# Row-wise infinity norm: the bulk loads move from SyncE's queue to GpSimd's, one packet per DMA engine

## The chip, the core and the metric

The kernel runs on one core of one Trainium2 chip. The metric is device time in microseconds (us) of one execution; lower is better. The core has a tensor, a vector (DVE), a scalar (ACT), a GpSimd (POOL) and a sync (SP) engine, and 16 DMA engines that move data between the memory of the chip (DRAM, HBM) and the on-chip memory of 128 partitions. Any of SP, ACT and POOL can issue a transfer; each of them feeds a queue of its own to the same 16 DMA engines.

## The reference

```
x: 8192 x 8192 float32, normally distributed
out = np.linalg.norm(x, ord=np.inf, axis=1)     # 8192 float32: max |x| of each row
```

Each of the 8192 output values is the largest absolute value of one row of 32 KB. The input is 268.4 MB, the output 32 KB.

## The kernel before

The rows are divided in two parts. Each partition has 64 rows in all; 48 of them are the bulk (`x_b`) and 16 are the tail (`x_t`, `n_tail` = 16).

**The bulk** (lines 65 to 72) is 24 loads, 6 (`A`) times 4 (`G`). Each fills one tile `t` of 128 partitions x 16384 float32: two whole rows per partition, 64 KB that lie together in DRAM, 8.39 MB in all. The load is issued by SP (line 68). One DVE instruction, `reduce_max` with absolute value (line 63, called from line 69), then reduces the tile to two values per partition in `r_bulk`. When all are done, ACT stores `r_bulk` (line 73).

**The tail** (lines 75 to 98) takes the other 16 rows of each partition, two rows (`B`) to a tile `t`, so 8 tiles. The list `TAIL` (lines 17 to 22) says in which pieces each row is loaded: 8 rows whole (32 KB per partition and piece), 5 rows in halves (16 KB), 2 rows in quarters (8 KB), and the last row in three quarters, one piece of 4 KB and two of 2 KB. That is 32 loads, all issued by SP (line 82), each followed by a DVE reduction of its piece (line 94 or 97, again through line 63) into `part` or, for the last row, into spare columns at the end of the tile. Before the last piece's own reduction DVE folds `part` into `r_tail` (line 87), which ACT stores (line 88). The last reduction (line 91) yields `r_fin`, which SP stores (line 99).

**What sets the order.** The tiles `t` of both parts come from one pool with three buffers (`BUFS` = 3, line 51). A load into a buffer waits for the reduction of what the buffer held: load number i waits for the reduction of tile i-3. The first tail tile therefore waits for bulk tile 21 (counting from 0), the second for bulk tile 22, and so on. Besides that, the framework signals the end of the DMAs issued by SP and ACT through eight semaphores in turn, and a DMA also waits until the previous user of its semaphore has landed. Instructions of one engine are issued in the order of the program: on SP all 24 bulk loads come ahead of the 32 tail loads.

In the text, T0 to T23 are the bulk tiles and R0 to R15 the tail rows. The loads of R0 and R1 fill one buffer, those of R2 and R3 the next.

Of the kernel before, what the change touches and what calls it, by code (L numbers as in the profile page):

```python
# [1 line left out]
logging.getLogger("concourse").setLevel(logging.ERROR)  # L3

# [1 line left out]

# [4 lines left out]

F32 = mybir.dt.float32
X = mybir.AxisListType.X

TAIL = (
    [[8192]] * 8
    + [[4096, 4096]] * 5
    + [[2048] * 4] * 2  # L20
    + [[2048, 2048, 2048, 1024, 512, 512]]
)


@with_exitstack
def kernel(
    ctx: ExitStack,
    tc: tile.TileContext,
    x: bass.AP,
    out: bass.AP,  # L30
    G: int = 4,
    B: int = 2,
    BUFS: int = 3,
):
    nc = tc.nc
    P = nc.NUM_PARTITIONS
    rows, cols = x.shape


    n_tail = len(TAIL)  # L40
    assert n_tail % B == 0
    n_bulk_rows = rows // P - n_tail
    assert n_bulk_rows % (G * B) == 0
    A = n_bulk_rows // (G * B)
    split = n_bulk_rows * P
    x_b = x[:split].rearrange("(a p n b) c -> a n p (b c)", p=P, a=A, n=G, b=B)
    out_b = out[:split].rearrange("(a p n b) -> p a (n b)", p=P, a=A, n=G, b=B)
    x_t = x[split:].rearrange("(p t b) c -> t p (b c)", p=P, b=B)
    out_t = out[split:].rearrange("(p t) -> p t", p=P)

    sbuf = ctx.enter_context(tc.tile_pool(name="sbuf", bufs=BUFS))
    outp = ctx.enter_context(tc.tile_pool(name="outp", bufs=1))

    k_last = len(TAIL[-1])
    r_bulk = outp.tile([P, A, G * B], F32)
    r_tail = outp.tile([P, n_tail], F32)
    r_fin = outp.tile([P, 1], F32)
    k_max = max(len(r) for r in TAIL[:-1])
    part = outp.tile([P, n_tail - 1, k_max], F32)
    nc.vector.memset(part[:], 0.0)  # L60

    def absmax(o, i):
        nc.vector.reduce_max(out=o, in_=i, axis=X, apply_absolute_value=True)  # L63

    for a in range(A):
        for n in range(G):
            t = sbuf.tile([P, B * cols + 16], F32, tag="t")
            nc.sync.dma_start(out=t[:, : B * cols], in_=x_b[a, n])  # L68
            absmax(
                r_bulk[:, a, n * B : (n + 1) * B],  # L70
                t[:, : B * cols].rearrange("p (b c) -> p b c", b=B),
            )
    nc.scalar.dma_start(out=out_b, in_=r_bulk[:])

    for i in range(0, n_tail, B):
        t = sbuf.tile([P, B * cols + 16], F32, tag="t")
        for j in range(B):
            r = i + j
            at = j * cols
            last = r == n_tail - 1  # L80
            for k, w in enumerate(TAIL[r]):
                nc.sync.dma_start(  # L82
                    out=t[:, at : at + w], in_=x_t[i // B][:, at : at + w]
                )
                if last and k == k_last - 1:

                    absmax(r_tail[:, : n_tail - 1], part[:])
                    nc.scalar.dma_start(
                        out=out_t[:, : n_tail - 1], in_=r_tail[:, : n_tail - 1]
                    )  # L90
                    absmax(r_fin[:], t[:, at : B * cols + k_last - 1])
                elif last:
                    absmax(
                        t[:, B * cols + k : B * cols + k + 1], t[:, at : at + w]
                    )
                else:
                    absmax(part[:, r, k : k + 1], t[:, at : at + w])
                at += w
    nc.sync.dma_start(out=out_t[:, n_tail - 1 :], in_=r_fin[:])


# [1 line left out]
_INS = ['x']  # L103
_OUTS = [((8192,), 'float32')]


# [23 lines left out]
```

## Time and profile before

| | us |
|---|---|
| median of 3 runs (629.82 to 629.88) | 629.88 |
| the profiled execution's own time | 629.88 |
| its span, first to last instruction | 628.1 |
| time around the span (629.88 - 628.1) | 1.78 |
| DVE busy | 552.7 |
| one bulk reduction (128x2 from 128x16384), 24 of them | 17.219 |
| one tail reduction of a whole row (128x8192), 8 of them | 8.677 |
| one tail reduction of half a row (128x4096), 10 of them | 4.412 |
| median of a bulk load from issue to landing | 40.7 |

The profile is that of one execution. A page of it gives the busy time of each engine, the span in 40 slices, the DMA queues (q1 carries what SP issues, q10 what ACT issues), and the chain of work that ended last, followed backwards. Other views are the timeline (instructions in order of time, with the idle time of the engine before each and what ended it), the waits (who waited for whom) and windows (rates and busy times in chosen stretches). The trace also holds a record of every DMA packet, with queue, size, start and length. `L63` is line 63 of the kernel; "SPq" is SP issuing a DMA. Input and tile names stand as `out<-in`.

### The profile page before, as it was taken

The page shows a single profiled execution, that of the slowest core. Times are in us where ns is not written, and L with a number is a line of the kernel's source. Part 1 is how long each engine was busy: PE and PEld are TensorE (multiplying, and loading weights), DVE is VectorE, ACT ScalarE, POOL GpSimd, SP SyncE. Part 2 cuts the span into 40 slices and gives each one's busy share as a digit, 9 for nine tenths or more (in the row PEclk, how much of TensorE's full clock was granted, in tenths as well). Part 3 has the DMA queues.
Part 4 walks back from the last instruction along what each step waited for, and adds up shares of the span by engine and source line. Part 5 has one row for each costly group of instructions (what it writes and reads, how often), then busy time and mean ns, then how long its engine had stood idle before and what let it go on. Part 6 is the DMA issues. An engine that isn't in the chain of part 4 may idle for free.

```text
span 628.1 us, 196 instructions
## 1 busy us (share of the span) xinstructions
DVE 552.7 (88%) x58; POOL 0.2 (0%) x4
## 2 busy tenths in 40 slices
DVE  0588988889988889888898888998889999999998
POOL 0000000000000000000000000000000000000000
DMA  9999999999999999999999999999999999999996
GB/s 401 413 455 413 455 413 455 413 455 413 455 413 455 409 459 413 455 413 455 413 455 413 455 413 455 413 455 413 455 405 430 434 435 432 420 432 432 424 426 274
DMA packets 9138, 268.49 MB, mean 427 GB/s; under 512 B 1968, under 2 KB 1968, under 8 KB 2352
## 3 DMA queue, kind: packets, MB, share of 16 engines
q1 hardware_dynamic: 8208, 268.44, 99.1%
q10 hardware_dynamic: 928, 0.03, 0.1%
q14 instruction: 2, 0.02, 0.0%
HBM read 268.44 MB, written 0.03 MB: 427 GB/s over the span
## 4 chain that ended last, share of the span: by engine, by line
DMA 64%; DVE 30%; another core or an unknown queue 4%; issue 1%; SPq 0%
DMA t<-in_x_dram 64%; DVE r_bulk L63 23%; DVE part L63 5%; DVE t L63 1%; SPq L82 0%; DVE r_fin L63 0%; SPq L68 0%
## 5 line engine op out<-in xcount | busy, mean ns | idle before, releaser
L63 DVE TENSOR_REDUCE r_bulk<-t 128x2 f32<-128x16384 f32 x24 | 413.3, 17219 | 70.5 <-DMA t<-in_x_dram 70.5
L63 DVE TENSOR_REDUCE part<-t 128x1 f32<-128x4096 f32 (+2 forms) x26 | 130.0, 5067 | 1.3 <-DMA t<-in_x_dram 1.3
L63 DVE TENSOR_REDUCE t<-t 128x1 f32<-128x2048 f32 (+2 forms) x5 | 8.6, 1746 | 0.4 <-DMA t<-in_x_dram 0.4
L60 DVE MEMSET part<- 128x60 f32 x1 | 0.1, 108 | 0.8 <-PEq L114 0.8
L63 DVE TENSOR_REDUCE r_fin<-t 128x1 f32<-128x517 f32 x1 | 0.7, 692 | 0.0
L63 DVE TENSOR_REDUCE r_tail<-part 128x15 f32<-128x60 f32 x1 | 0.2, 216 | 0.0
L114 POOL MEMSET const-bfloat16-1.0<- 128x1 bf16 x1 | 0.1, 101 | 0.0
L114 POOL MEMSET const-uint8-127<- 128x1 uint8 x1 | 0.1, 101 | 0.0
L114 POOL MEMSET const-float32-0.0<- 128x1 f32 x1 | 0.1, 98 | 0.2 <-issue 0.2
L114 POOL MEMSET const-float32-1.0<- 128x1 f32 x1 | 0.1, 98 | 0.0
## 6 DMA issues: line engine op xcount, KB each, us to landing
t<-in_x_dram SPq DMA_DIRECT2D x8, 4096.0 KB, 37.0
t<-in_x_dram SPq DMA_DIRECT2D x10, 2048.0 KB, 30.4
t<-in_x_dram SPq DMA_DIRECT2D x11, 1024.0 KB, 24.6
t<-in_x_dram SPq DMA_DIRECT2D x1, 512.0 KB, 15.9
t<-in_x_dram SPq DMA_DIRECT2D x2, 256.0 KB, 13.2
t<-in_x_dram SPq DMA_DIRECT2D x24, 40.7
out_dram<-r_bulk ACTq DMA_DIRECT2D x1, 24.0 KB, 57.9
out_dram<-r_tail ACTq DMA_DIRECT2D x1, 7.5 KB, 5.6
```

The source lines that it names most:

```text
L60: nc.vector.memset(part[:], 0.0)
L63: nc.vector.reduce_max(out=o, in_=i, axis=X, apply_absolute_value=True)
L114: nc = _bacc.Bacc("TRN2", target_bir_lowering=False, num_devices=1)
```

## The change

Line 68, the load of the bulk, is issued by GpSimd in place of SP, and with the option `single_packet=True`. The option asks that all descriptors that one DMA engine gets of one load (here those of 8 partitions) make one packet. Nothing else is edited: the tail loads stay on SP, the stores stay where they are, the shapes, the buffers and the reductions are the same.

```
     for a in range(A):
         for n in range(G):
             t = sbuf.tile([P, B * cols + 16], F32, tag="t")
-            nc.sync.dma_start(out=t[:, : B * cols], in_=x_b[a, n])
+            nc.gpsimd.dma_start(
+                out=t[:, : B * cols], in_=x_b[a, n], single_packet=True
+            )
             absmax(
                 r_bulk[:, a, n * B : (n + 1) * B],
                 t[:, : B * cols].rearrange("p (b c) -> p b c", b=B),
```

More of the change, by code (lines that the diff above doesn't have):

```diff
@@ L67 @@
             t = sbuf.tile([P, B * cols + 16], F32, tag="t")
-            nc.sync.dma_start(out=t[:, : B * cols], in_=x_b[a, n])
+            nc.gpsimd.dma_start(
+                out=t[:, : B * cols], in_=x_b[a, n], single_packet=True
+            )
             absmax(
```

## The prediction

> **What bounds the kernel now.** I read the page first: span and engines, the slices, the queues, the chain.
>
> ```profile
> span 628.1 us, 196 instructions
> DVE 552.7 (88%) x58; POOL 0.2 (0%) x4
> ...
> GB/s 401 413 455 413 455 413 455 413 455 413 455 413 455 409 459 413 455 413 455 413 455 413 455 413 455 413 455 413 455 405 430 434 435 432 420 432 432 424 426 274
> ...
> q1 hardware_dynamic: 8208, 268.44, 99.1%
> q10 hardware_dynamic: 928, 0.03, 0.1%
> ...
> DMA 64%; DVE 30%; another core or an unknown queue 4%; issue 1%; SPq 0%
> ```
>
> Look at q1: one queue keeps the 16 DMA engines busy for 99.1% of the span, and the rate is level from the second slice to the last but one. DVE is 88% busy, so it has slack, but only 75 us in 628. The transfers are the bound. The bulk is read from the timeline, whose last column says what DVE waited for:
>
> ```profile
> 0.73 116.98 SPq L68 DMA_DIRECT2D t<-in_x_dram  x8
> ...
> 22.83 17.22 DVE L63 TENSOR_REDUCE r_bulk<-t 128x2 f32<-128x16384 f32 x1 [21.91 <-DMA t<-in_x_dram]
> 42.11 17.22 DVE L63 TENSOR_REDUCE r_bulk<-t 128x2 f32<-128x16384 f32 x1 [2.06 <-DMA t<-in_x_dram]
> ```
>
> DVE starts each tile when it lands and then idles about 2.1 us. The hand-over to the tail is in the same view:
>
> ```profile
> 428.83 17.22 DVE L63 TENSOR_REDUCE r_bulk<-t 128x2 f32<-128x16384 f32 x1 [2.14 <-DMA t<-in_x_dram]
> 446.07 165.44 SPq L82 DMA_DIRECT2D t<-in_x_dram  x32
> 448.11 17.22 DVE L63 TENSOR_REDUCE r_bulk<-t 128x2 f32<-128x16384 f32 x1 [2.06 <-DMA t<-in_x_dram]
> 467.49 17.22 DVE L63 TENSOR_REDUCE r_bulk<-t 128x2 f32<-128x16384 f32 x1 [2.15 <-DMA t<-in_x_dram]
> 484.62 60.23 DVE L63 TENSOR_REDUCE part<-t 128x1 f32<-128x8192 f32 x7
> ```
>
> T23 starts on DVE at 467.49, T0 at 22.83: 444.66 / 23 = 19.333 us per load of 8.389 MB, 433.9 GB/s. SP issues the first tail load at 446.07, just as T21's reduction frees its buffer (428.83 + 17.22), while T22 is landing and T23 is queued. After T23 DVE is the late one for a while: it goes from 484.62 without a gap through seven rows.
>
> How DVE's lateness is worked off: R0's packets end at 476.7 (packet records), DVE takes it at 484.6, so it is 7.9 us behind; the rows land 9.7 us apart and take 8.68, about 1 us regained per row, so at R7 DVE waits again. Behind T23 DVE idles only 0.38 + 0.56 + 0.38 + 0.15 + 0.20 = 1.7 us until it ends at 625.74. That 1.7 us is all the lateness that T23 can gain without moving the end.
>
> **The rates in windows**, for what a packet costs (last column GB/s: the bulk, then pieces of 32, 16 and 8 KB):
>
> ```profile
> 177.48:254.73 77.25, 68.88 (x4) 0.00 (x0) 1.00 1.00 434
> ...
> 488.00:540.00 52.00, 52.00 (x7) 0.00 (x0) 1.00 1.01 434
> 550.00:590.00 40.00, 39.44 (x10) 0.00 (x0) 1.00 1.01 432
> 594.00:619.00 25.00, 24.81 (x12) 0.00 (x0) 1.00 1.01 426
> ```
>
> The packet records say the same more finely. Each bulk load is 128 packets of 64 KB, 8 per engine, of 2.418 us each; 32 KB packets take 1.213. Twice 1.213 less 2.418 leaves 8 ns that a packet (or a descriptor, here the same) costs beyond its bytes.
>
> **Part 1: issue moves from SP to POOL.** 24 issues of 0.328 us (7.9 us) and their 21 waits for buffers leave SP for POOL, whose own work is four memsets of 0.1 us that end at 0.43. In steady state nothing of it is on the path: a load is issued 40.7 us before it lands, 19.3 of which are its own transfer and some 20 the queue ahead. POOL may take up to 20 us per load before a DMA engine runs dry. POOL's slowness would have to pass that cover, 60 times SP's row, to cost anything.
>
> A rule that speaks against it: the Trainium skill ("SBUF — State Buffer", the box on DVE blocking DMA) says that GpSimd can't write its descriptors while DVE runs a two-port fast mode. The 17.219 us for 16384 elements, 1.05 ns each, look like one element per step, and no row here shows such a lock. Were it held for a whole reduction, 17.2 us would still lie within the cover.
>
> The first load has no cover. SP issues it at 0.73, its first packet starts at 1.75 (records): 1.02 us. No row shows POOL doing this. From below: 0, it is as fast. From above: three loads are issued back to back, and if POOL prepares all before the first moves, three times SP's 1.02, so +2.0. I take +1.0, twice SP's time, because descriptors now come from a program. It shifts every landing, the end too: all of it is on the path.
>
> The skill's page "DMA: Bandwidth & Descriptors" (Specifications) gives about 1 us to the first byte for GpSimd's path and 0.6 for SP's; by that the term would be +0.4 and the forecast 629.6.
>
> **Part 2: one packet per engine.** Eight packets become one. If the 8 ns belong to the packet, 7 x 8 ns x 24 loads = 1.3 us go; if to the descriptor, none. Bounds of the bulk's rate: at best -1.3 (the bytes alone set the rest). At worst, the lowest rate that a full queue shows here, 426 GB/s of the 8 KB pieces: 24 x 19.333 = 464.0 us x (434/426 - 1) = +8.7. The nearest row is the bulk's own, same bytes, same runs, so I stay by it and take the middle of 0 and -1.3, -0.65.
>
> Against it speaks the skill's same page (Latency and other measured facts): engines 7 and 15 are usually slower, with a guess that descriptor rings in on-chip memory, which only GpSimd's path has, load their ports. In this trace all 16 engines finish each load within 0.9 us of each other (T23: 466.2 to 467.0), with no drift over 24 loads; there is no such ring here, and no row prices it.
>
> **Part 3: two queues meet at the hand-over.** Before, R0 stood behind T23 in one queue. Now T23 waits in POOL's queue and R0 in SP's. How the engines share is visible in the bulk's store on ACT (L73): issued at 484.74, 57.9 us to landing. It has 6 x 128 runs of 32 bytes and 16 semaphore writes, 49 small packets per engine; 57.9 / 49 = 1.18 us, one 32 KB packet of SP between any two. The engines alternate packet by packet. So T23 as one packet, once begun, can't be cut. The engines begin it between 446.83 and 447.68; SP's R0, issued at 446.07, is there 1.02 later, 447.09, when 10 of 16 have begun T23. On the others one packet of R0, 1.21 us, may pass first. T23 is then 1.2 us late, within the 1.7 us. Cost 0. SP's later loads are released by DVE as before, and SP's longest wait behind the store (23.2 us, to 542.66) has cover: the engines have work until 544.8 + 4.8 (R8's first half) = 549.6, less 1.02 for the issue, so 5.9 us. Stores, reductions and the end don't change.
>
> **Sum.** Against the profiled run's own 629.88 (628.1 + 1.78 around it; equal to the median): +1.0 - 0.65 + 0 = +0.35, 630.2. Its own range: -1.3 + 0 to 0 + 2.0, 628.6 to 631.9.
>
> **Rivals.**
> - *Interleaving (slower).* The option doesn't act, as each load has 128 descriptors in all, or each descriptor stays a packet. Place: 447. T23's eight packets alternate with R0's and R1's: 8 x 2.42 + 8 x 1.21 = 29.0 us in place of 19.3, so T23 is 9.7 us late; if two packets are already begun, 7.3. Less DVE's 1.7 us of idle: +5.6 to +8.0. With +1.0 for the start and no packet gain: 636.5 to 638.9. It decides once T23 lands over 1.7 us late. For it: the store shows strict alternation. Against: the option is meant for this, and 8 descriptors per engine are few.
> - *A lower rate on GpSimd's queue (slower).* From 432 to 426 GB/s over the bulk, the 16 and 8 KB rows: +2.1 to +8.7, plus 1.0: 633 to 639.6. For it: no row shows this queue. Against: equal bytes and runs, and engines that are already the limit.
> - *The full packet gain with a quick start (faster).* -1.3 + 0: 628.6, hardly beyond what can be told. Nothing in the profile allows more, as start, 268 MB and end stay.
>
> **Numbers.** A measurement of this kernel tells from no change about 0.2%, 1.26 us. Forecast 0.50 (faster 0.03, same 0.33, slower 0.14, as its upper end passes 631.1), faster rival 0.15 (0.10 beyond the bound, 0.05 within), lower rate 0.20, interleaving 0.15. Faster 0.13, same 0.38, slower 0.49. Signs are mixed, so the likeliest case's own range, 628.6 to 631.9, stands beside the whole: 628.5 to 637.5, which cuts the upper ends of the two slow rivals.
>
> **What would show it.** A queue of POOL's with 201.3 MB, q1 with 67.1. First reduction at 23.8 in place of 22.83 (start). Reductions 19.28 us apart if the packet gain is full, 19.33 if none, above that a slow queue. T23's start on DVE 19.3 us after T22's, and idle time behind it as before; with interleaving 27 to 29 us after, and no DVE idle to the end. I am wrong if POOL's first issue costs several us, if one DMA engine lags, or if DVE's tail loses its gaps.

## The result, and the profile after

The changed kernel takes **639.1 us** (639.01 to 639.29) against 629.88: ratio 1.0145, 95% interval 1.0127 to 1.0163, so 9.2 us slower. The forecast was 630.2 with a range to 637.5. The profiled execution took 639.08.

The page of the changed kernel, the same parts as were shown of before:

```profile
span 637.0 us, 204 instructions
DVE 552.1 (87%) x58; POOL 13.0 (2%) x28
...
GB/s 383 407 461 416 440 444 412 461 395 461 444 412 461 395 461 444 412 461 395 461 432 424 457 399 461 420 436 449 426 409 428 414 430 428 422 429 430 423 426 89
...
q0 software_dynamic: 3456, 201.33, 73.1%
q1 hardware_dynamic: 4752, 67.11, 24.7%
...
DMA 53%; DVE 46%; issue 1%; DVEq 0%; PEldq 0%
```

The bulk's 201.3 MB now go through a queue of their own, q0. The rate stays as level as before, and DVE has no more work. Yet DVE's share of the chain that ended last has gone from 30% to 46%: the end is now set by DVE, not by the transfers. The last slice, 89 GB/s, says the same: most of it passes after the last load has landed.

The timeline shows where that came from (last column: DVE's idle time and what ended it):

```profile
1.25 1.70 POOL L68 DMA_DIRECT2D t<-in_x_dram  x3 [0.80 <-PEq L127]
23.70 17.22 DVE L63 TENSOR_REDUCE r_bulk<-t 128x2 f32<-128x16384 f32 x1 [22.77 <-DMA t<-in_x_dram]
...
446.98 167.25 SPq L84 DMA_DIRECT2D t<-in_x_dram  x32
449.01 17.22 DVE L63 TENSOR_REDUCE r_bulk<-t 128x2 f32<-128x16384 f32 x1 [2.06 <-DMA t<-in_x_dram]
478.34 8.69 DVE L63 TENSOR_REDUCE part<-t 128x1 f32<-128x8192 f32 x1 [12.11 <-DMA t<-in_x_dram]
486.95 17.21 DVE L63 TENSOR_REDUCE r_bulk<-t 128x2 f32<-128x16384 f32 x1
504.07 121.04 DVE L63 TENSOR_REDUCE part<-t 128x1 f32<-128x8192 f32 x25
```

Three things are to be seen. The first reduction starts 0.87 us later (23.70, was 22.83). From T0 to T22 the spacing is (449.01 - 23.70) / 22 = 19.332 us, as before. Then, at the hand-over, DVE idles 12.11 us where it idled 2.15, and takes a tail row (R0) ahead of T23; after that it works without a gap to the end.

The account: +0.87 (start) + 9.96 (12.11 - 2.15) - 1.67 (the gaps behind T23 that are gone) = 9.16. DVE's work is 0.6 shorter, the part behind its last reduction 0.26 longer (637.0 - 634.38, was 628.1 - 625.74) and the time around the span 0.30 longer, which makes 9.1 in all; 9.2 were measured.

The packet records of one DMA engine (rebuilt by joining each packet's end to the next one's start; POOL's packets of 64 KB as P, SP's of 32 KB as S, start times) show why T23 is late:

```
445.4 P  447.8 P  450.2 P  452.6 S  453.8 P  456.2 S  457.4 P  459.9 S  461.1 P  463.5 S ...
```

The first packet is T22's last, the next two are T23's, and from then on R0 and T23 take turns (on six of the 16 engines after one packet of T23). T23's packets end at 476.40; 19.33 us behind T22's (448.58) they would have ended at 467.9.

### The profile page after: what moved, and what is told of

It is laid out like the page before. It is cut to its first block, busy times and chain, and to the rows that moved or that the text cites. A ratio compares the mean times of both kernels' runs of the same rounds, so it can differ in the third digit from the quotient of the medians.

```text
span 637.0 us, 204 instructions
## 1 busy us (share of the span) xinstructions
DVE 552.1 (87%) x58; POOL 13.0 (2%) x28
## 3 DMA queue, kind: packets, MB, share of 16 engines
q0 software_dynamic: 3456, 201.33, 73.1%
## 4 chain that ended last, share of the span: by engine, by line
DMA 53%; DVE 46%; issue 1%; DVEq 0%; PEldq 0%
DMA t<-in_x_dram 53%; DVE r_bulk L63 24%; DVE part L63 20%; DVE t L63 1%; DVE r_fin L63 0%; DVE r_tail L63 0%; DVEq L63 0%; PEldq L127 0%
## 5 line engine op out<-in xcount | busy, mean ns | idle before, releaser
L68 POOL DMA_DIRECT2D t<-in_x_dram x24 | 12.8, 533 | 415.2 <-DVE r_bulk L63 414.4
```

What stands on the lines that cost most here:

```text
L68: nc.gpsimd.dma_start(out=t[:, : B * cols], in_=x_b[a, n], single_packet=True)
```

## The experiments

**Theory after this result:** two queues share each DMA engine descriptor by descriptor, whatever the option says; T23 lands 8 to 10 us late; the tail gives DVE no slack to make it up. **Rivals:** the option itself costs; the swapped order on DVE costs; GpSimd's queue is slower in itself; any hand-over costs this.

### e1: without the option

```
-            nc.gpsimd.dma_start(out=..., in_=x_b[a, n], single_packet=True)
+            nc.gpsimd.dma_start(out=..., in_=x_b[a, n])
```

> The changed kernel without the one-packet option; nothing else differs. Theory (the option doesn't keep T23 whole, two queues share an engine descriptor by descriptor whatever it says): 639.1 within 0.4 us, T23's last packet at 476.4, R0 and T23 alternating, DVE idle 12.1 us ahead of R0, reductions 19.33 us apart. Rival (the option itself costs or saves, in the rate of the bulk or at the hand-over): more than 1 us away from 639.1, another spacing of the reductions or another end of T23's packets.

Measured 639.15 us (ratio 1.0147, 1.0132 to 1.0163). T23's packets end 27.80 us after T22's, in the changed kernel 27.82; DVE idles 12.08:

```profile
478.55 8.69 DVE L63 TENSOR_REDUCE part<-t 128x1 f32<-128x8192 f32 x1 [12.08 <-DMA t<-in_x_dram]
```

The option changes nothing that these runs can tell.

### e2: T23 ahead of R0 on DVE

```
+    with tc.issue_after(last_bulk.ins):     # DVE's tail work behind T23's reduction
         for i in range(0, n_tail, B):
```

> The changed kernel, with DVE made to reduce T23 ahead of R0 as in the kernel before; the two queues still share the engines at the hand-over. Theory (T23 lands 8.5 us late because R0 and T23 alternate): DVE starts T23 at about 476.9, 9.4 us later than before, and the end comes 1.5 us ahead of the changed kernel's: 637.6. Rival (the swapped order on DVE is what costs, the sharing is nearly harmless): 631 to 632.

Measured 638.95 us (1.0145, 1.0128 to 1.0162). Its hand-over in the timeline:

```profile
448.84 17.22 DVE L63 TENSOR_REDUCE r_bulk<-t 128x2 f32<-128x16384 f32 x1 [2.08 <-DMA t<-in_x_dram]
477.90 17.22 DVE L63 TENSOR_REDUCE r_bulk<-t 128x2 f32<-128x16384 f32 x1 [11.84 <-DMA t<-in_x_dram]
```

T23 starts 29.06 us after T22, 9.73 late, and that alone makes the time (630.72 of e7, where nothing shares, + 9.73 - 1.67 = 638.8); the order on DVE, which the framework's scheduler had turned by itself, adds nothing that these runs can tell (639.1 and 638.95). My 637.6 was 1.3 too low: T23's packets end at 476.23, but the four bytes that signal its end are written until 477.45. In the records that write takes a turn of its own: it comes behind another packet of SP's, of 1.21 us.

### e3 and e4: one load held back, a failed test

```
+                if r == 0:     # R0's load waits for T22's reduction
+                    tc.add_manual_dep(ld.ins, bulk_red[-2].name, <wait>)
```

> The changed kernel, with R0's load made to wait until DVE has reduced T22 (one tile later than its buffer is free), so that T23 isn't cut; DVE's order stays swapped, R0 ahead of T23. If the swapped order alone is enough: T23's packets end at 468, R0's at about 478, DVE idles some 12 us until R0 and the time is 638.5 to 639.5, as if nothing had been undone. If the sharing alone is the cause: 631.

> Both undone: R0's load waits for T22's reduction, and DVE reduces T23 ahead of R0. The loads of the bulk are still on GpSimd with the one-packet option. Theory (only the hand-over and the start cost): T23 starts on DVE at 468.4, 19.3 us after T22, the engines pause under 0.5 us between T23 and R0, and the time is 629.9 + 0.9 (start) + up to 0.5 = 630.8 to 631.3. Rival (GpSimd's queue costs something by itself, in rate or in the tail): above 632.

Measured 639.12 (e3; 1.0146, 1.0131 to 1.0161) and 638.66 us (e4; 1.0139, 1.0124 to 1.0154). In both, SP still issues a tail load at the old time (446.90 and 447.00): R0 and R1 share a buffer, the scheduler put R1's load ahead, and it shared the engines in R0's place. T23 starts at 478.12 in e4. Neither run undid the sharing, so neither speaks on the theory.

### e5: both loads held back

```
-                if r == 0:
+                if r <= 1:
```

> As e3, but both loads that share the first tail buffer, R0's and R1's, wait until DVE has reduced T22 (in e3 and e4 only R0's waited, R1's was issued ahead of it at 447 and shared the engines in its place, so neither was a test of the sharing). The scheduler then puts T23 ahead of R0 on DVE by itself. Theory (the sharing at the hand-over is what costs): SP's first issue at 466.3, T23 starts on DVE at 468.4, DMA engines pause under 0.5 us, DVE's idle gaps in the tail come back, 629.9 + 0.9 (start) + 0 to 0.5 = 630.8 to 631.3. Rival (GpSimd's queue costs by itself, in its rate or in what follows it): above 632, towards 639.

Measured 633.78 us (1.0059, 1.0042 to 1.0076): over half of the loss is gone, but it is 2.5 above the upper end of what I expected. Timeline:

```profile
466.23 148.84 SPq L86 DMA_DIRECT2D t<-in_x_dram  x32
468.34 17.22 DVE L63 TENSOR_REDUCE r_bulk<-t 128x2 f32<-128x16384 f32 x1 [2.14 <-DMA t<-in_x_dram]
485.48 43.05 DVE L63 TENSOR_REDUCE part<-t 128x1 f32<-128x8192 f32 x5
529.29 8.69 DVE L63 TENSOR_REDUCE part<-t 128x1 f32<-128x8192 f32 x1 [0.77 <-DMA t<-in_x_dram]
```

T23 is on time, and DVE's gaps in the tail are back, larger than before: the transfers bind again, but late ones. In windows (DMA share and GB/s last) the two stretches behind T23's end, first here, then in e7 (one queue, below):

```profile
466.00:470.00 4.00, 1.86 (x2) 0.00 (x0) 1.00 0.72 254
470.00:474.00 4.00, 4.00 (x1) 0.00 (x0) 1.00 0.90 385
```

```profile
466.00:470.00 4.00, 1.86 (x2) 1.04 (x2) 1.00 0.84 360
470.00:474.00 4.00, 4.00 (x1) 0.00 (x0) 1.00 0.99 426
```

SP issues at 466.23, the first packet of R0 starts at 467.25, and the engines finish T23 from 466.96 on: some ran dry. The packet records say how much: all engines have finished T23 by 467.9, the last one begins R0 only at 469.5, at least 1.6 us later, and the first packets take 1.3 to 2.3 us in place of 1.21. A row needs all 16 engines; R7's packets end at 548.4, in e7 at 545.65. The loss is that of the last engine: its start 1.7 us late (in e7 the last one begins R0 at 467.8) and its first packet up to 1.1 us longer, 2.8 of the 3.4 us by which the two profiled executions differ (634.04 and 630.66). So e5 shows that T23 is on time without the sharing, and that most of what is left is the price of the wait that I put in.

### e6: hand-over in the middle of the bulk

```
+            if a < 3:
                 nc.gpsimd.dma_start(..., single_packet=True)
+            else:
+                nc.sync.dma_start(out=t[:, : B * cols], in_=x_b[a, n])
```

> The first 12 bulk loads on GpSimd with the option, the other 12 and the tail on SP: the hand-over is at T11 and T12, in the middle of the bulk. Theory (what costs is DVE's lateness, and only where it can't be worked off): T11 lands 17 to 19 us late since its packets alternate with T12's of equal size, DVE is then that much behind, regains 2.1 us per tile and is on time again by about T21, the engines stay busy: 629.9 + 0.9 (start) + 0 to 1 = 630.8 to 631.8. Rivals: any hand-over between two queues costs its 8 to 10 us, 639 or more; GpSimd's queue costs in proportion to what it loads, 634 to 635.

Measured 634.03 us (1.0067, 1.0052 to 1.0082). Timeline, T10, then T11 with the seven tiles behind it, then T19:

```profile
216.90 17.22 DVE L63 TENSOR_REDUCE r_bulk<-t 128x2 f32<-128x16384 f32 x1 [2.07 <-DMA t<-in_x_dram]
255.79 137.10 DVE L63 TENSOR_REDUCE r_bulk<-t 128x2 f32<-128x16384 f32 x8 [21.67 <-DMA t<-in_x_dram]
393.63 17.22 DVE L63 TENSOR_REDUCE r_bulk<-t 128x2 f32<-128x16384 f32 x1 [0.73 <-DMA t<-in_x_dram]
```

T11 is 19.5 us late (236.26 in e7), twice the lateness of T23, and DVE works it off within eight tiles: here lateness costs nothing by itself. What it does cost is the cover of one load: T14's waits for T11's reduction (273.0), and T13's packets end from 273.65 to 274.5. Engines run dry again (four begin T14 only at 276.1 to 276.5), and T23 starts at 470.94, in e7 at 468.26. So my bound of 1 us was too low, by the same effect as in e5. That GpSimd's queue costs by bytes loaded would fit this time too; e7 rules that out.

### e7: all loads on GpSimd

```
-                nc.sync.dma_start(out=t[:, at : at + w], in_=x_t[...])
+                nc.gpsimd.dma_start(out=t[:, at : at + w], in_=x_t[...])
```

> All loads, the tail's too, on GpSimd, so one queue and no hand-over. Theory: T23 starts 19.3 us after T22, the tail as before, 629.9 + 0.9 = 630.8 to 631.5 (0.533 us of POOL per issue are hidden). Rival (GpSimd's queue itself is slower): 634 and up, and more than in e6.

Measured **630.72 us** (1.0013, 1.0004 to 1.0023). One queue, and the loss is gone but for the start:

```profile
448.90 17.22 DVE L63 TENSOR_REDUCE r_bulk<-t 128x2 f32<-128x16384 f32 x1 [2.06 <-DMA t<-in_x_dram]
468.26 17.22 DVE L63 TENSOR_REDUCE r_bulk<-t 128x2 f32<-128x16384 f32 x1 [2.14 <-DMA t<-in_x_dram]
485.40 60.23 DVE L63 TENSOR_REDUCE part<-t 128x1 f32<-128x8192 f32 x7
546.11 43.35 DVE L63 TENSOR_REDUCE part<-t 128x1 f32<-128x8192 f32 x9 [0.48 <-DMA t<-in_x_dram]
```

This is the timeline of before, 0.8 us later line by line. GpSimd's queue is as fast as SP's, in bulk and in small pieces.

### e8: hand-over one tile later

```
-                nc.sync.dma_start(
+                (nc.gpsimd if i == 0 else nc.sync).dma_start(     # R0, R1 on GpSimd
```

> The changed kernel, with R0's and R1's loads on GpSimd too, so that the hand-over comes one tile later: R0 and R1 share the engines with R2 and R3, and T23 is whole. Theory: R0 lands 7.3 to 9.7 us late, at 485.4 to 488.3, but DVE is busy with T23 until 485.5 in any case, so DVE loses 0 to 2.8 us and has 1.7 to give: 629.9 + 0.9 + 0 to 1.1 = 630.8 to 631.9. Rival (the lateness of the load counts in full wherever the hand-over is): 637 and up.

Measured 640.98 us (1.0176, 1.0161 to 1.0191), 9 above my expectation. Timeline from T23 on:

```profile
468.19 17.22 DVE L63 TENSOR_REDUCE r_bulk<-t 128x2 f32<-128x16384 f32 x1 [2.14 <-DMA t<-in_x_dram]
486.43 8.69 DVE L63 TENSOR_REDUCE part<-t 128x1 f32<-128x8192 f32 x1 [1.02 <-DMA t<-in_x_dram]
505.80 121.05 DVE L63 TENSOR_REDUCE part<-t 128x1 f32<-128x8192 f32 x25 [10.69 <-DMA t<-in_x_dram]
```

R0 came as I had worked out (486.4). I had followed R0 alone: R1 stands behind it in the same queue and shares with R3, so DVE waits 10.69 us for R1. The theory's own sum holds: 630.72 (e7) + 1.02 + 10.69 - 1.67 = 640.8.

### e9 and e10: T23 in small descriptors, with and without the option

Both start from e2. `last` is true for T23; `max_dma_last_dim` is the most bytes that a descriptor may move.

```
             nc.gpsimd.dma_start(
                 out=t[:, : B * cols], in_=x_b[a, n],
+                single_packet=True,      # e10: not on T23
+                max_dma_last_dim=16384 if last else 65536,
             )
```

> As e2 (T23 ahead of R0 on DVE), with only T23's load made of descriptors of 16 KB in place of 64, 32 per engine, and with the one-packet option on it. If the option makes an engine's share one packet that isn't cut: T23 lands within about 1 us of its time, 631 to 632. If the option doesn't bear on how two queues share an engine: as e10. Something between, near 639: a packet is bounded by its bytes (64 KB).

> As e9 without the option on T23's load. Theory (the engines alternate descriptor by descriptor): each of T23's 32 descriptors of 0.61 us is followed by one of SP's of 1.21, R0 to R3 pass ahead of T23's end, T23's packets end at about 502 in place of 468, DVE idles from 466 to then and ends 33 to 34 us later than with one queue: 663 to 666. Rival (the engines share by bytes, or by load): as the changed kernel, near 639.

Measured 661.33 us (e9; 1.0498, 1.0467 to 1.0528) and 660.81 (e10; 1.0489, 1.0459 to 1.052). T23's start on DVE, e9 and then e10:

```profile
500.79 17.22 DVE L63 TENSOR_REDUCE r_bulk<-t 128x2 f32<-128x16384 f32 x1 [33.87 <-DMA t<-in_x_dram]
```

```profile
499.99 17.22 DVE L63 TENSOR_REDUCE r_bulk<-t 128x2 f32<-128x16384 f32 x1 [33.87 <-DMA t<-in_x_dram]
```

The same bytes in four times as many descriptors make T23 not 9.7 but 32 us late: each descriptor of 0.61 us lets one of 1.21 pass. The turns go by descriptor, not by bytes or loads, and the option makes no difference: DVE's wait is the same to the hundredth. The two profiled executions (661.55 and 660.79) are 0.76 us apart, and T22 already starts 0.80 apart (449.70 and 448.90), ahead of the hand-over.

The time of e10 is 2.2 below my expectation of 663 to 666: T23's packets end at 498.31, where I had put 502. I had let one of SP's packets follow each of the 32 descriptors, but the first four or five of an engine passed before SP's first packet was there (450.33).

### e11 and e12: T23 as four small loads, with and without the option

These too start from e2.

```
+            step = 4 if last else 1
+            for h in range(step):
+                nc.gpsimd.dma_start(out=t[h::step, ...], in_=x_b[a, n][h::step],
+                                    single_packet=True)      # e12: not on T23
```

> As e2, with T23's load split in four loads of every fourth partition, 32 descriptors of 64 KB each (2 per engine), the one-packet option on each: the option's limit, if it counts the descriptors of the whole load (128 in the changed kernel), is no longer passed. If the option then keeps an engine's two descriptors together: two of T23's packets in a row for each of R0's, T23 is 4 to 5 us late in place of 8.5 to 9.7, 633 to 635. Theory (no effect on the sharing): strict alternation, 638.5 to 640.

> As e11 without the option on T23's four loads: strict alternation, T23 8.5 to 9.7 us late, 638.5 to 640. If it isn't near the changed kernel's time, the four loads cost something by themselves, and e11 is to be read against this one.

Measured 641.66 us (1.0183, 1.0153 to 1.0212) and 641.88 (1.0186, 1.0157 to 1.0216). T23's start, e11 and then e12:

```profile
480.81 17.22 DVE L63 TENSOR_REDUCE r_bulk<-t 128x2 f32<-128x16384 f32 x1 [14.56 <-DMA t<-in_x_dram]
```

```profile
480.99 17.22 DVE L63 TENSOR_REDUCE r_bulk<-t 128x2 f32<-128x16384 f32 x1 [14.74 <-DMA t<-in_x_dram]
```

The option has no effect on loads of 32 descriptors either, so a limit between 32 and 128 descriptors of the whole load isn't what kept it from acting. In e11's records, too, a packet of SP's stands between the two descriptors that an engine has of one load (P at 455.62, S at 458.04, P at 459.25). Both times are above what I expected, 2.7 and 2.9 above e2: four loads have four end signals per engine, three turns more (3 x 1.21 = 3.6 at most).

## Why the prediction was wrong, point by point

- **What bounds the kernel** was right, and so was the 1.7 us that T23 may be late. Behind T23 the bound passes to DVE, whose remaining work of 156.7 us (17.2 + 130.0 + 0.2 + 8.6 + 0.7, by the page of before) then runs without a gap.
- **Part 1, the start**: +1.0 forecast, +0.87 measured. GpSimd issues at 1.25 (SP: 0.73), and its first packet starts 1.36 us later (SP: 1.02). The 0.4 that I worked out from the Trainium skill ("DMA: Bandwidth & Descriptors", Specifications) is half of it; the run decides. In steady state GpSimd's 0.53 us per issue were hidden, as said. No row shows the port lock that the Trainium skill ("SBUF — State Buffer", the box on DVE blocking DMA) warns of. The changed kernel hardly tests it, as GpSimd issues in DVE's pauses (at 41.22, DVE idle from 40.92 to 42.98). In e7 it issued under DVE's reductions (two in 1.05 us from 485.78), as fast as in the pauses, and the tail kept its time.
- **Part 2, the packet gain**: -0.65 forecast, 0 measured (19.332 us per load). The 8 ns go with the descriptor, or nothing was joined; the runs don't separate these, and the trace has 3456 records on q0 with the option and without it (e1). Nor did a DMA engine lag, though the Trainium skill ("DMA: Bandwidth & Descriptors", Latency and other measured facts) calls engines 7 and 15 usually slower: the engines finished T22 within 0.9 us of each other.
- **Part 3 is the step that failed**: "So T23 as one packet, once begun, can't be cut", at cost 0. I had read from ACT's store that the engines alternate packet by packet, and then took the option at its word that eight descriptors would be one packet. No row showed that; the row at hand was one of strict alternation, single descriptor against single descriptor. What the runs showed in its place: T23 is cut after each of its descriptors, at a price of 9.7 us in place of 0 (29.06 us from T22 to T23 in place of 19.33, e2), and e1, e9 with e10, and e11 with e12 show that the option doesn't bear on the sharing. The step has a second error, which by itself would have favoured the forecast: R0 was to be at the engines 1.02 us after its issue, when 10 of 16 had begun T23; its first packet started 3.5 us after, when all 16 had (the last at 448.58).
- **The rival "interleaving"** had the mechanism, the place and nearly the price: 29.0 us between T22 and T23, measured 29.06 (e2); 636.5 to 638.9, measured 639.1. It had 0.15, though the only row on sharing spoke for it, and the range cut its upper end. It took 9.7 us for the upper bound, for the case that none of T23's packets had begun; one or two had, but the end signal takes a turn too, and so 9.7 was the value.
- That the scheduler would turn T23 and R0 on DVE was not foreseen; e2 shows that little hangs on it.
- The rival of a slower queue fell with e7; the faster one fell with the start of +0.87 and the spacing of 19.332.

Left open: whether the option does anything on this chip. Only its effect on sharing and rate was tested, and no row shows that it reached the descriptors at all.

## What to carry to other kernels

At each of the three hand-overs tried here (T23 to R0, T11 to T12, R0 to R2) a stream that was split over two queues lost its order where they met: both parts landed together, and the first one was late. Count the turns (descriptors and end signals of the other queue), and ask at that place how much lateness the consumer can work off: in the middle of the bulk 19.5 us cost nothing by themselves, in the tail all but 1.7 of 10 were lost. Where a flag is meant to prevent what a row of the trace shows, the row is the better forecast until a run shows the flag at work.

## What the runs showed of the hardware that was not expected

- Descriptors of two queues took turns one by one on an engine, at each pair of sizes tried: 64 KB against 32, 32 against 32 (e8), 16 against 32 (e10). The write that signals a load's end takes a turn too (e2: 1.2 us after the data).
- SP's first packet in the changed kernel started 3.5 us after its issue (446.98 to 450.48), behind one or two of T23's packets of 64 KB. In e10, where T23's packets are of 16 KB and four or five went ahead, it was 3.5 again (446.85 to 450.33), and in e6 and e8 3.4: at busy engines the lead is a time rather than a number of packets. At idle engines it was 1.02 (the start of before; e5, 466.23 to 467.25). Why it differs is open.
- A queue that runs dry costs more than the gap. In e5 and e6 the next load's first packet started only 0.3 us after the first engine was free (467.25 against 466.96; 273.99 against 273.65), and yet the transfers behind it were 2.7 us late: some engines began 1.6 to 2 us after the last one was free, and the first packets ran up to 90% (e5) and 40% (e6) longer. Why is open.
